# A decoder layer in split float32: two output units interleaved, weight-sum copies moved from SyncE to GpSimd, seven raw places

## The chip, the cores and the metric

The kernel runs on one core of one Trainium2 chip. The metric is the device time of one execution in microseconds (us). The core has TensorE (matmuls; PE in the profile, PEld for its weight loads), VectorE (DVE), ScalarE (ACT), GpSimd (POOL) and SyncE (SP). SyncE, ScalarE and GpSimd also issue DMAs, each in the order of its own queue; 16 DMA engines carry them out.

## What is computed

The reference is one decoder layer on 2048 tokens of width 1024, in float32:

```python
proj = rmsnorm(x, mix_norm_g) @ w_in
q, k, v, g, u = split(proj)                  # 4 heads of 128; u: 4 groups of 128 channels
y_ret  = silu(g) * head_rmsnorm(retention(rope(q), rope(k), v))
y_pool = pool_mixer(u, pool_w, pool_scale)   # trailing means over 2, 4, 8, 16 tokens, minus the token
x = x + concat(y_ret, y_pool) @ w_out
x = x + cross_attn(rmsnorm(x), mem_n, wq, wkv, wo)        # 4 heads, 256 memory tokens
x = x + conv_glu_ffn(rmsnorm(x), w_up, conv_w, w_down)    # width 2816, conv of 3
return rmsnorm(x, final_norm_g)
```

## The kernel before, in words

**Arithmetic.** Channels lie on the 128 partitions, tokens along the free axis. The tokens go in two blocks (`b` = 0, 1) of 1024, each in two halves of 512. A float32 operand is split into a high and a low part (`split`: ScalarE writes the high part at L259 or L262, VectorE the low part at L242 or L251), and each product takes three matmuls (`passes`, L267 to L269).

**Units.** `unit` (L313) makes one output tile of 128 channels: it splits a raw weight of 1024 columns into two pairs (tiles 0 to 3 and 4 to 7 of the depth), takes two PSUM banks, one for each token half, and runs four quarters of 12 matmuls: first half of the depth for both token halves, then the second, after which `evac` takes the bank away. After each quarter it draws one step of `behind[0]` (a retention or a norm running beside) and of `under[0]` (the weight sums). There are five banks. Raw weights land in `raws`, places in R and S; pairs lie in `prs`, places in Q. `new_raw` and `new_pair` use these in turn.

**Order of work.** Folded weights are computed first (the products of the attention and pooling matrices, left in Md, VWd and WPd in DRAM) while the tokens of block 0 are loaded and squared; GpSimd makes four small sums there for the memory's norm. Then, for each block: the values; the heads and pools; eight output units (L1867 on), which add to the tokens and form the next norm; the attention (16 token tiles, L856 on); eight units for its output (L1911 on), which in block 0 also load and split the tokens of block 1 (`fetch_x`, `load_x`), with the value weights of block 1 after the last. The feed-forward part runs at the end in rounds.

**Products of seven.** Block 1's heads and the whole feed-forward part multiply 2x2 blocks with seven products in place of eight. That needs sums of weight blocks, made by DMA: `weight_sums` (L939) has 42 jobs (8 in Ad for the heads, 22 in Ud, 12 in Dd). A job takes four blocks a11, a12, a21, a22 and fills d0 to d3 in DRAM: four plain copies (L950, on SyncE), then four accumulating DMAs on GpSimd: d2 += a22 and d0 += a21 (L952, L953), d1 += d2 (L956), d3 += d1 (L959). The copies are tied by `tc.issue_after(fetched[0].ins)`: they stand in SyncE's queue behind the weight load that was fetched last when they were drawn. Each `yield` is one step drawn by a unit, by an attention tile (`pace` steps, L920; `pace` is b + 1) or by the value part of block 1.

**Heads of block 1** (`head_projections`, L1514) are eight members of seven products. The last member holds pools 0 and 1; head 3's retention runs beside it. During this part R gives five raw places of 512 columns, and S is a second holder of pairs (`more`), so that there are five pairs. Finished tiles are split into `mix[k]` by `settle`: 0 to 3 are the heads, 4 to 7 the pools. Head 3's result lies in the buffer E and is split into X (part of G); tile 4 is split into a new E, which is the buffer that head 3's result leaves. The first output unit of block 1 takes the tiles in the order 7, 6, 0, 1, 2, 5, 3, 4, the others in the order 0 to 7.

**Who sets the order.** The program is fully unrolled. Each engine's queue is ordered ahead of time by a scheduler; only the last five products are ordered by hand. Dependencies are kept by semaphores, and a queue is then worked through in order.

Of the kernel before, what the change touches and what calls it, by code (L numbers as in the profile page):

```python
# [136 lines left out]
def trunk(ctx, tc, xT, memT, pos, w_qkgu, w_v, wkv, wqT, wo, wout_r, wout_p, poolT, w_up, w_dn, vecs, consts, outT):  # L137
# [16 lines left out]
    def new_e(dtype):  # L154
        return Arena(cp.tile([P, 4 * T], dtype, tag="E", name=nm("E")), 0, 4, T)

    def new_s(dtype):
        return cp.tile([P, 2 * T], dtype, tag="S", name=nm("S"))

    B = Joined(Arena(G, 16 * T, 12, T), new_e(F32R))  # L160

# [4 lines left out]
    TT = Arena(cp.tile([P, TEMPS * TW], F32, tag="T", name="T"), 0, TEMPS, TW)  # L166
    R = cp.tile([P, 3 * T], F32, tag="R", name="R")
    Q = cp.tile([P, 3 * T], F32R, tag="Q", name="Q")
    S = new_s(F32)
    raws = Places([(R, j * T) for j in range(3)] + [(S, j * T) for j in range(2)], T)  # L170
    prs = Places([(Q, j * T) for j in range(3)], T)
    vc = cp.tile([P, vecs.shape[1]], F32, tag="vecs", name="vecs")
    cs_t = cp.tile([P, consts.shape[1]], F32, tag="consts", name="consts")
# [138 lines left out]

    def unit(raw, rhs, evac, order=range(KT)):  # L313


        hs = raw if isinstance(raw, list) else pairs(raw)
        ps = [mmps() for _ in range(NS)]
        for h in range(2):
            for s in range(NS):
                for j, k in enumerate(order[4 * h : 4 * h + 4]):  # L320
                    w = [hs[k // 4][:, i, k % 4 * P : (k % 4 + 1) * P] for i in range(2)]
                    passes(ps[s], w, rhs(k, s), h + j == 0, h == 1 and j == 3)
                next(behind[0], None)
                quarter[0] += 1
                if not slow[0] or quarter[0] % 2:
                    next(under[0], None)
                if h == 1:
                    evac(s, ps[s])

    def load_tile(src, room=None):  # L330
        raw = new_raw() if room is None else room.f
# [214 lines left out]
    def fetch_x(b, k):  # L546

        out = []
        for s in range(NS):
            out.append(TT.take())  # L550
            sp.dma_start(out[s].f[:, :SUB], xT[k * P : (k + 1) * P, b * T + s * SUB : b * T + (s + 1) * SUB])
        return out

    def load_x(k, s_acc, got):
# [301 lines left out]
    def attention(sums, beside, pace):  # L856


        scl, nscl = (smp.tile([P, 8], F32, tag="scl", name=nm("scl"), bufs=2) for _ in range(2))
        low, high, far = B.arenas[0].take(KT), B.arenas[0].take(KT // 2), B.arenas[1].take(KT // 2)  # L860
        tables = [low, None, new_z(F32R).take(KT)]
        prob = [([high, far], [high.r, far.r]), ([low], [low.r[:, : 4 * T], low.r[:, 4 * T :]])]

        def load_m(hp):

            out = mw[hp]
            for kp in range(KT // 2):
                raw = new_raw()
                fetched[0] = sp.dma_start(raw.rearrange("p (k n) -> p k n", k=2), Md[hp, 2 * kp : 2 * kp + 2].rearrange("k p n -> p k n"))
                if hp == 0 and kp == 0:  # L870

                    out += [(pr[:, 0], pr[:, 1]) for pr in pairs(raw)]
                    yield
                    continue
                for i in range(2):
                    u = tables[2 * hp].r[:, (2 * kp + i) * T : (2 * kp + i + 1) * T]
                    split(raw[:, i * SUB : (i + 1) * SUB], u[:, :SUB], u[:, SUB:])
                    out.append((u[:, :SUB], u[:, SUB:]))
                yield

        def turn(pt, t, e):
            tp = aux()
            for j in range(4):
                pe.transpose(tp[:, j * P : (j + 1) * P], e.f[:, j * P : (j + 1) * P], ident)
            hi, lo = (r.rearrange("p (k t) -> p k t", t=T)[:, :, t * P : (t + 1) * P] for r in pt[1])
            turned.append(act.activation(hi, tp.rearrange("p (k t) -> p k t", k=4), AF.Copy))
            tt(dve, lo, tp.rearrange("p (k t) -> p k t", k=4), hi.bitcast(F32), ALU.subtract)
            e.free()

        turned.clear()  # L890
        mw = [[], []]
        for _ in load_m(0):
            pass
        more_m = load_m(1)
        late = []
        for i in range(2 * KT):
            hp, t = divmod(i, KT)
            ps = mmps()
            for k in range(KT):
                x2 = [X[:, 2 * k + j, t * P : (t + 1) * P] for j in range(2)]  # L900
                passes(ps, x2, mw[hp][k], k == 0, k == KT - 1)
            if i == 0:
                rn, _, _ = norm_tables(sums, wide=False)
                ts(dve, scl, rn, 1.0 / 16.0, ALU.mult)
                ts(dve, nscl, rn, -1.0 / 16.0, ALU.mult)
            mx, sm = small(2), small(2)
            dve.reduce_max(out=mx, in_=ps.rearrange("p (h m) -> p h m", h=2), axis=AX.X)
            ts(dve, mx, mx, nscl[:, t : t + 1], ALU.mult)
            e = TT.take()
            for j in range(2):  # L910
                act.activation(e.f[:, j * NMEM : (j + 1) * NMEM], ps[:, j * NMEM : (j + 1) * NMEM], AF.Exp,
                               bias=mx[:, j : j + 1], scale=scl[:, t : t + 1], accum_out=sm[:, j : j + 1])
            dve.reciprocal(sm, sm)
            for j in range(2):
                ej = e.f[:, j * NMEM : (j + 1) * NMEM]
                ts(dve, ej, ej, sm[:, j : j + 1], ALU.mult)
            if len(late) == 2:
                turn(*late.pop(0))
            late.append((prob[hp], t, e))
            for _ in range(pace):  # L920
                next(under[0], None)
            if i < KT - 2:
                next(more_m, None)
            else:
                for _ in range(pace):
                    next(beside, None)

        def end():
            for one in late:
                yield turn(*one)  # L930

        return prob, end()
# [6 lines left out]
    def weight_sums():  # L939

        jobs = [((w_qkgu[a], w_qkgu[c]), 0, 4, Ad[p]) for p, (a, c) in enumerate(PAIRS)]
        jobs += [((w_up[f], w_up[f + NF]), 0, 4, Ud[f]) for f in range(NF)]
        for at, (k0, n) in enumerate(ROUNDS):
            jobs += [((w_dn[2 * j], w_dn[2 * j + 1]), k0, n, Dd[at, j]) for j in range(KT // 2)]
        for w, k0, n, to, in jobs:
            a11, a12, a21, a22 = (block(w, i // 2, i % 2, k0, n) for i in range(4))
            d = [to[i][:, : n * P] for i in range(4)]
            with tc.issue_after(fetched[0].ins):
                for i, a in ((2, a21), (0, a11), (1, a11), (3, a12)):
                    sp.dma_start(d[i], a)  # L950
            yield
            pool.dma_start(d[2], a22, accum_op=ALU.add, max_dma_last_dim=2048)  # L952
            pool.dma_start(d[0], a21, accum_op=ALU.add, max_dma_last_dim=2048)  # L953
            yield
            yield
            pool.dma_start(d[1], d[2], accum_op=ALU.add, max_dma_last_dim=2048)  # L956
            yield
            yield
            pool.dma_start(d[3], d[1], accum_op=ALU.add, max_dma_last_dim=2048)  # L959

    class Round:

# [551 lines left out]
    def head_projections(b, v, rb, tabs, t1, t2, z3, z4):  # L1514
# [1 line left out]

        nonlocal raws, prs
        pieces, far = B.arenas[0], new_e(F32)
        more = new_s(F32R)
        raws = Places([(R, j * SUB) for j in range(5)], SUB)  # L1520
        side = Arena(R, 5 * SUB, 1, SUB).take().f
        prs = Places([(Q, j * T) for j in range(3)] + [(more, j * T) for j in range(2)], T)
        t3 = pieces.take(4)
        todo, ready, mix, gates, outs, tables = [], [], [None] * KT, {}, {}, []

# [202 lines left out]
        while ready:  # L1728
            settle(True)
        assert all(u is not None for u in mix) and far.room() == 4  # L1730
        spare = new_s(F32)
        raws = Places([(R, j * T) for j in range(3)] + [(spare, j * T) for j in range(2)], T)
        prs = Places([(Q, j * T) for j in range(3)], T)
        return mix, spare

    def rows_norm(s_acc):
        rn = smp.tile([P, 8], F32, tag="rn", name=nm("rn"), bufs=3)
# [84 lines left out]
    for b in range(NB):  # L1822
# [19 lines left out]
        else:  # L1842
# [14 lines left out]
            tabs = [TT.take() for _ in range(2)]  # L1857
            for i in range(2):
                sp.dma_start(tabs[i].f[:, :SUB], rope_d[i])
            mix, S = head_projections(b, v, rb, tabs, t1, t2, z3, z4)  # L1860
        for r in rb:
            r.free()
        slow[0] = False

        xs = [TT.take() for _ in range(NS)]
        ahead = fetch_x(b, 0)
        for n in range(KT):  # L1867
            raw = new_raw()
            sp.dma_start(raw[:, :SUB], wout_r[n].rearrange("p k c -> p (k c)"))
            fetched[0] = sp.dma_start(raw[:, SUB:], WPd[n].rearrange("p k c -> p (k c)"))  # L1870
            got, ahead = ahead, fetch_x(b, n + 1) if n + 1 < KT else None
            unit(raw, lambda k, s: [r[:, s * SUB : (s + 1) * SUB] for r in mix[k][1]], add_residual(b, n, xs, got=got), (0, 2, 3, 1, 4, 6, 7, 5) if b == 0 else (7, 6, 0, 1, 2, 5, 3, 4) if n == 0 else range(KT))
        for u, _ in mix:
            if u is not None:
                u.free()
# [21 lines left out]
        def opening(room, wv):  # L1897
# [1 line left out]
            for r in room:  # L1899
                r.free()  # L1900
            for kp in range(KT // 2):
                wv.append(value_weights(kp))
                if kp:
                    yield

# [57 lines left out]
    for _ in under[0]:  # L1963
        pass
    both[0] = False
    raws = Places([(R, j * SUB) for j in range(6)] + [(S, j * SUB) for j in range(4)], SUB)
    prs = Places([(Q, j * T) for j in range(3)] + [(B.arenas[1].t, j * T) for j in range(4)], T)
    AA = Places([(Z.t, j * (T + EDGE)) for j in range(4)], T + EDGE)
    CC = Places([(Z.t, 4 * EDGE + j * T) for j in range(4, 8)], T)
# [111 lines left out]
```

## Time and profile before

| | |
|---|---|
| three runs | 2477.16, 2478.46, 2483.21 us; median 2478.46 |
| profiled execution | 2478.89 us; its span 2477.0 us |
| mean granted TensorE clock | 0.992 |
| bytes moved by DMA | 501.56 MB, 202 GB/s |
| DMA queues, share of the 16 engines | SyncE (q1) 52.4%, GpSimd (q0) 10.8%, ScalarE (q10) 3.3% |

The span goes from the first to the last instruction. The lines of the profile name engine, line, operation, `out<-in` by the program's names, and count; `[x <-y]` is idle time of the engine before, and what ended it. SPq, POOLq and ACTq are DMA issues. A busy TensorE is not one at its peak: matmuls overlap, so the count in a window tells the rate.

### The profile page before, as it was taken

Reading aid. Unit: us, or ns where it says so; the run is one execution under the profiler, and the core shown is the slowest. Engines: PE = TensorE matmul, PEld = TensorE weight load, DVE = VectorE, ACT = ScalarE, POOL = GpSimd, SP = SyncE. Lnnn points to the kernel's source line nnn. Section 1 sums busy time; section 2 is a strip of 40 time slices with the busy share of each in tenths; the row PEclk is TensorE's granted clock in tenths of the full one; section 3 lists DMA queues with packets and bytes.
Section 4 is the critical chain, followed back from the end, with each engine's and each line's share of the span. In section 5 each row is a group of like instructions: output and inputs, shape, how many; then the busy total and the mean of one; then the engine's idle time right before and its main releaser. Section 6 shows DMA issues by size and latency. Waiting matters only on the chain.

```text
span 2477.0 us, 33287 instructions
## 1 busy us (share of the span) xinstructions
PE 2422.2 (98%) x11294; PEld 2018.0 (81%) x11294; DVE 1730.7 (70%) x2969; ACT 1283.2 (52%) x2303; POOL 206.9 (8%) x272
## 2 busy tenths in 40 slices
PE   6999999999999999999999999999999999999997
PEld 6888888878788877888888888888888888888886
DVE  8645576564676675575678876897667688867876
ACT  6333423443444443434655565665555677666663
POOL 1010111101001131200000010020000000000000
PEclk9999999999999999999999999999999999999998
DMA  8363789727748898966468665665546468768951
GB/s 315 95 167 115 222 209 244 226 51 223 219 125 199 203 258 246 250 204 249 145 198 278 210 190 158 218 222 169 161 154 216 136 223 302 246 189 280 344 171 69
DMA packets 274459, 501.56 MB, mean 202 GB/s; under 512 B 28784, under 2 KB 58096, under 8 KB 274288
## 3 DMA queue, kind: packets, MB, share of 16 engines
q1 hardware_dynamic: 225584, 428.11, 52.4%
q0 software_dynamic: 24192, 43.00, 10.8%
q10 hardware_dynamic: 24512, 28.32, 3.3%
q8 instruction: 89, 1.46, 0.2%
q14 instruction: 82, 0.67, 0.1%
HBM read 398.13 MB, written 187.17 MB: 236 GB/s over the span
## 4 chain that ended last, share of the span: by engine, by line
PE 88%; DMA 5%; DVE 4%; ACT 1%; issue 1%; SPq 0%; POOLq 0%; POOL 0%; ACTq 0%; DVEq 0%
PE mm L267 28%; PE mm L269 28%; PE mm L268 27%; DMA T<-xT 1%; DVE T L242 1%; DMA T<-Xd 1%; DVE Z L242 1%; PE aux L342 1%; PE aux L268 1%; PE aux L267 1%; PE aux L269 1%; PE aux L777 0%; DVE Q L242 0%; DMA T<-pos 0%; DMA Hd<-T 0%
## 5 line engine op out<-in xcount | busy, mean ns | idle before, releaser
L267 PE MATMUL mm<-G,Q 128*128 128x512 f32 (+1 forms) x1720 | 663.2, 386 | 23.5 <-ACT Q L259 14.6
L269 PE MATMUL mm<-G,Q 128*128 128x512 f32 (+1 forms) x1720 | 660.8, 385 | 6.3 <-DVE Q L242 6.1
L268 PE MATMUL mm<-G,Q 128*128 128x512 f32 (+1 forms) x1592 | 609.8, 383 | 0.2 <-DVE G L242 0.2
L268 PE MATMUL mm<-G,E 128*128 128x512 f32 x1084 | 421.6, 389 | 0.0
L267 PE MATMUL mm<-G,E 128*128 128x512 f32 x1084 | 420.2, 390 | 0.0
L269 PE MATMUL mm<-G,E 128*128 128x512 f32 x1084 | 419.2, 389 | 0.0
L267 PEld LDWEIGHTS mm<-G,Q 128*128 128x128 f32 x1720 | 326.6, 190 | 88.9 <-ACT Q L259 15.9
L269 PEld LDWEIGHTS mm<-G,Q 128*128 128x128 f32 x1720 | 326.4, 190 | 70.7 <-DVE Q L242 8.4
L268 PEld LDWEIGHTS mm<-G,Q 128*128 128x128 f32 x1592 | 302.1, 190 | 57.3 <-DVE G L242 1.5
L242 DVE TENSOR_TENSOR Z<-Z,mm 128x512 f32<-128x512 f32 x296 | 201.4, 681 | 101.2 <-PE mm L269 101.0
L251 DVE SCALAR_TENSOR_TENSOR Z<-Z,vecs 128x1024 f32<-128x1024 f32 x176 | 224.5, 1279 | 50.0 <-ACT Z L1104 46.4
L267 PEld LDWEIGHTS mm<-G,E 128*128 128x128 f32 x1084 | 203.5, 188 | 42.4 <-ACT Z L1186 0.3
L269 PEld LDWEIGHTS mm<-G,E 128*128 128x128 f32 x1084 | 203.5, 188 | 42.3
L268 PEld LDWEIGHTS mm<-G,E 128*128 128x128 f32 x1084 | 203.5, 188 | 42.1
L1041 ACT ACTIVATE E<-R 128x512 fp32r<-128x512 f32 (+1 forms) x165 | 101.5, 615 | 142.8 <-PE mm L268 135.3
L242 DVE TENSOR_TENSOR T<-T 128x512 f32<-128x512 f32 (+3 forms) x224 | 152.9, 688 | 23.2 <-ACT T L382 11.1
L242 DVE TENSOR_TENSOR Q<-R,Q 128x512 fp32r<-128x512 f32 x153 | 106.1, 696 | 74.5 <-ACT Q L259 50.8
L242 DVE TENSOR_TENSOR G<-T,G 128x512 fp32r<-128x512 f32 (+1 forms) x181 | 119.0, 673 | 42.5 <-ACT G L990 30.5
L1041 ACT ACTIVATE Q<-R 128x512 fp32r<-128x512 f32 (+1 forms) x157 | 96.9, 618 | 99.6 <-PE mm L268 73.8
L1104 ACT ACTIVATE Z<-Z,vecs 128x1024 f32<-128x1024 f32 x88 | 109.2, 1242 | 35.5 <-DVE Z L242 34.5
L990 ACT ACTIVATE G<-T 128x512 fp32r<-128x512 f32 x157 | 95.9, 625 | 54.5 <-DMA T<-Hd 27.3
L242 DVE TENSOR_TENSOR E<-R,E 128x512 fp32r<-128x512 f32 (+1 forms) x131 | 87.4, 671 | 51.2 <-ACT E L1041 42.3
(308 smaller groups left out, 3666.6 us busy)
## 6 DMA issues: line engine op xcount, KB each, us to landing
T<-Gd SPq DMA_DIRECT2D x168, 256.0 KB, 4.3
Gd<-Z SPq DMA_DIRECT2D x110, 256.0 KB, 2.7
R<-Ud SPq DMA_DIRECT2D x106, 256.0 KB, 2.7
Ud<-w_up SPq DMA_DIRECT2D x88, 256.0 KB, 6.1
R<-w_up SPq DMA_DIRECT2D x80, 256.0 KB, 3.0
S<-Ud SPq DMA_DIRECT2D x70, 256.0 KB, 2.8
T<-xT SPq DMA_DIRECT2D x64, 256.0 KB, 4.2
Gd<-T SPq DMA_DIRECT2D x56, 256.0 KB, 3.3
```

The costliest lines, as they stand in the source:

```text
L242: return eng.tensor_tensor(out=out, in0=a, in1=b, op=op)
L251: dve.scalar_tensor_tensor(out=out, in0=a, scalar=s, in1=b, op0=op0, op1=op1)
L267: pe.matmul(ps, lh, rh, start=start, stop=False, skip_group_check=more)
L268: pe.matmul(ps, lh, rl, start=False, stop=False, skip_group_check=more)
L269: latest[0] = pe.matmul(ps, ll, rh, start=False, stop=stop, skip_group_check=more)
L342: pe.matmul(ps[:, t : t + 1], ap, one, start=True, stop=more is None)
L990: act.activation(hi, x, AF.Copy)
L1041: act.activation(p2[:, 0, :w], self.raw[i].f[:, :w], AF.Copy)
L1104: act.activation(self.c[g].f, a[:, 2:], AF.Identity, bias=cb[:, f : f + 1], scale=cw[2][:, f : f + 1])
```

## The change

Copies and adds of a weight sum are both issued by GpSimd, with no tie to a SyncE load; up to four jobs are drawn in turn, four steps a job in place of five. The attention draws `4 - pace` steps a tile: 3 in block 0 (before: 1), 2 in block 1 (as before). S is split into two holders: during the heads of block 1 the first holds one pair (four in all), the second two raw places (seven in all). The first two output units of block 1 run together: four banks, first half of the depth for unit 0 and unit 1, then the second half; tiles in the order 6, 7, 0, 1, 2, 4, 5, 3; their weights are loaded in that order by four DMAs each; unit 0's pairs are split ahead, unit 1's second pair when its turn comes. The loads of block 1's value weights are tied behind the last token load.

```diff
-    def new_s(dtype):
-        return cp.tile([P, 2 * T], dtype, tag="S", name=nm("S"))
+    def new_s(dtype, at):
+        return cp.tile([P, T], dtype, tag=f"S{at}", name=nm("S"))
...
     def unit(raw, rhs, evac, order=range(KT)):
-        hs = raw if isinstance(raw, list) else pairs(raw)
-        ps = [mmps() for _ in range(NS)]
+        units([raw if isinstance(raw, list) else pairs(raw)], rhs, [evac], order, lambda k: k)
+
+    def units(weights, rhs, evacs, order, at):
+        ps = [[mmps() for _ in range(NS)] for _ in weights]
         for h in range(2):
-            for s in range(NS):
...
+            for hs, evac, banks in zip(weights, evacs, ps):
+                if callable(hs[h]):
+                    hs[h] = hs[h]()
+                for s in range(NS):
+                    for j, k in enumerate(order[4 * h : 4 * h + 4]):
+                        w = [hs[at(k) // 4][:, i, at(k) % 4 * P : (at(k) % 4 + 1) * P] for i in range(2)]
+                        passes(banks[s], w, rhs(k, s), h + j == 0, h == 1 and j == 3)
+                    next(behind[0], None)
+                    quarter[0] += 1
+                    if not slow[0] or quarter[0] % 2:
+                        next(under[0], None)
+                    if h == 1:
+                        evac(s, banks[s])
...
-            sp.dma_start(out[s].f[:, :SUB], xT[...])
+            fetched[0] = sp.dma_start(out[s].f[:, :SUB], xT[...])
...
-            for _ in range(pace):
+            for _ in range(4 - pace):
                 next(under[0], None)
...
-        for w, k0, n, to, in jobs:
+
+        def sums(w, k0, n, to):
             a11, a12, a21, a22 = (block(w, i // 2, i % 2, k0, n) for i in range(4))
             d = [to[i][:, : n * P] for i in range(4)]
-            with tc.issue_after(fetched[0].ins):
-                for i, a in ((2, a21), (0, a11), (1, a11), (3, a12)):
-                    sp.dma_start(d[i], a)
+            def add(at, a):
+                pool.dma_start(d[at], a, accum_op=ALU.add, max_dma_last_dim=2048)
+            for i, a in ((2, a21), (0, a11), (1, a11), (3, a12)):
+                pool.dma_start(d[i], a, max_dma_last_dim=2048)
             yield
-            pool.dma_start(d[2], a22, accum_op=ALU.add, max_dma_last_dim=2048)
-            pool.dma_start(d[0], a21, accum_op=ALU.add, max_dma_last_dim=2048)
+            add(2, a22)
+            add(0, a21)
             yield
+            add(1, d[2])
             yield
-            pool.dma_start(d[1], d[2], accum_op=ALU.add, max_dma_last_dim=2048)
-            yield
-            yield
-            pool.dma_start(d[3], d[1], accum_op=ALU.add, max_dma_last_dim=2048)
+            add(3, d[1])
+
+        live, jobs = [], [sums(*j) for j in jobs]
+        while jobs or live:
+            if jobs:
+                live.append(jobs.pop(0))
+            for g in list(live):
+                if next(g, True) is not None:
+                    live.remove(g)
+                yield
...
-        more = new_s(F32R)
-        raws = Places([(R, j * SUB) for j in range(5)], SUB)
+        more = new_s(F32R, 0)
+        raws = Places([(R, j * SUB) for j in range(5)] + [(S[1], j * SUB) for j in range(2)], SUB)
...
-        prs = Places([(Q, j * T) for j in range(3)] + [(more, j * T) for j in range(2)], T)
+        prs = Places([(Q, j * T) for j in range(3)] + [(more, 0)], T)
...
+        first = 0
+        if b:
+            first, order = 2, (6, 7, 0, 1, 2, 4, 5, 3)
+            weights, evacs = [], []
+            for n in range(first):
+                raw = new_raw()
+                r = raw.rearrange("p (k c) -> p k c", c=P)
+                for at, w in ((0, WPd[n][:, 2:4]), (2, wout_r[n][:, 0:3]), (5, WPd[n][:, 0:2]), (7, wout_r[n][:, 3:4])):
+                    fetched[0] = sp.dma_start(r[:, at : at + w.shape[1]], w)
+
+                def weight_half(h, raw=raw):
+                    pr = new_pair()
+                    split(raw[:, h * SUB : (h + 1) * SUB], pr[:, 0], pr[:, 1])
+                    return pr
+
+                weights.append([weight_half(0), lambda one=weight_half: one(1)])
+                evacs.append(add_residual(b, n, xs, got=ahead))
+                ahead = fetch_x(b, n + 1)
+            weights[0][1] = weights[0][1]()
+            units(weights, mixed, evacs, order, order.index)
+        for n in range(first, KT):
...
-                wv.append(value_weights(kp))
+                with tc.issue_after(fetched[0].ins):
+                    wv.append(value_weights(kp))
```

More of the change, by code (lines that the diff above doesn't have):

```diff
@@ L168, in trunk @@
     Q = cp.tile([P, 3 * T], F32R, tag="Q", name="Q")
-    S = new_s(F32)
-    raws = Places([(R, j * T) for j in range(3)] + [(S, j * T) for j in range(2)], T)
+    S = [new_s(F32, j) for j in range(2)]
+    raws = Places([(R, j * T) for j in range(3)] + [(r, 0) for r in S], T)
     prs = Places([(Q, j * T) for j in range(3)], T)
@@ L313, in unit @@
     def unit(raw, rhs, evac, order=range(KT)):
-        hs = raw if isinstance(raw, list) else pairs(raw)
-        ps = [mmps() for _ in range(NS)]
+        units([raw if isinstance(raw, list) else pairs(raw)], rhs, [evac], order, lambda k: k)
+    def units(weights, rhs, evacs, order, at):
+        ps = [[mmps() for _ in range(NS)] for _ in weights]
         for h in range(2):
-            for s in range(NS):
[L320 to L328, printed above, removed]
+            for hs, evac, banks in zip(weights, evacs, ps):
[11 more added lines that the diff above has]
+                        evac(s, banks[s])
     def load_tile(src, room=None):
@@ L550, in fetch_x @@
             out.append(TT.take())
-            sp.dma_start(out[s].f[:, :SUB], xT[k * P : (k + 1) * P, b * T + s * SUB : b * T + (s + 1) * SUB])
+            fetched[0] = sp.dma_start(out[s].f[:, :SUB], xT[k * P : (k + 1) * P, b * T + s * SUB : b * T + (s + 1) * SUB])
         return out
@@ L1730, in head_projections @@
         assert all(u is not None for u in mix) and far.room() == 4
-        spare = new_s(F32)
-        raws = Places([(R, j * T) for j in range(3)] + [(spare, j * T) for j in range(2)], T)
+        S[0] = new_s(F32, 0)
+        raws = Places([(R, j * T) for j in range(3)] + [(r, 0) for r in S], T)
         prs = Places([(Q, j * T) for j in range(3)], T)
-        return mix, spare
+        return mix
     def rows_norm(s_acc):
@@ L1859, in trunk @@
                 sp.dma_start(tabs[i].f[:, :SUB], rope_d[i])
-            mix, S = head_projections(b, v, rb, tabs, t1, t2, z3, z4)
+            mix = head_projections(b, v, rb, tabs, t1, t2, z3, z4)
         for r in rb:
@@ L1866, in trunk, with mixed @@
         ahead = fetch_x(b, 0)
-        for n in range(KT):
+        def mixed(k, s):
+            return [r[:, s * SUB : (s + 1) * SUB] for r in mix[k][1]]
+        first = 0
[17 more added lines that the diff above has]
+        for n in range(first, KT):
             raw = new_raw()
@@ L1871, in trunk @@
             got, ahead = ahead, fetch_x(b, n + 1) if n + 1 < KT else None
-            unit(raw, lambda k, s: [r[:, s * SUB : (s + 1) * SUB] for r in mix[k][1]], add_residual(b, n, xs, got=got), (0, 2, 3, 1, 4, 6, 7, 5) if b == 0 else (7, 6, 0, 1, 2, 5, 3, 4) if n == 0 else range(KT))
+            unit(raw, mixed, add_residual(b, n, xs, got=got), (0, 2, 3, 1, 4, 6, 7, 5) if b == 0 else range(KT))
         for u, _ in mix:
@@ L1965, in trunk @@
     both[0] = False
-    raws = Places([(R, j * SUB) for j in range(6)] + [(S, j * SUB) for j in range(4)], SUB)
+    raws = Places([(R, j * SUB) for j in range(6)] + [(r, j * SUB) for r in S for j in range(2)], SUB)
     prs = Places([(Q, j * T) for j in range(3)] + [(B.arenas[1].t, j * T) for j in range(4)], T)
```

## The prediction

> **What bounds the kernel now.** I read the page first: the engine shares, the slices, the chain that ended last.
>
> ```profile
> span 2477.0 us, 33287 instructions
> PE 2422.2 (98%) x11294; PEld 2018.0 (81%) x11294; DVE 1730.7 (70%) x2969; ACT 1283.2 (52%) x2303; POOL 206.9 (8%) x272
> DMA  8363789727748898966468665665546468768951
> PE 88%; DMA 5%; DVE 4%; ACT 1%; issue 1%; SPq 0%; POOLq 0%; POOL 0%; ACTq 0%; DVEq 0%
> ```
>
> TensorE is the bound, and 54.8 us are all it stands idle. So the change can win only where TensorE is not full, and I cut the span into stages (the view by windows; columns: length, busy time and count of PE, PEld, DVE, ACT, POOL, then granted clock, DMA share, GB/s).
>
> ```profile
> 0.00:60.00 60.00, 39.24 (x267) 37.25 (x268) 51.35 (x90) 40.93 (x62) 9.16 (x12) 0.94 0.89 316
> 25.00:60.00 35.00, 25.55 (x183) 23.86 (x182) 35.00 (x57) 28.58 (x45) 2.64 (x3) 0.90 0.86 288
> 60.00:580.00 520.00, 515.61 (x2620) 437.22 (x2619) 315.29 (x671) 196.84 (x421) 50.20 (x61) 1.00 0.61 166
> 620.00:640.00 20.00, 15.62 (x55) 11.90 (x55) 10.74 (x17) 8.02 (x14) 2.84 (x4) 0.83 1.08 272
> 640.00:913.00 273.00, 270.59 (x1337) 225.86 (x1336) 189.63 (x403) 132.30 (x273) 38.78 (x47) 1.00 0.73 193
> 913.90:936.50 22.60, 16.08 (x62) 10.76 (x61) 18.59 (x56) 9.73 (x33) 12.49 (x15) 0.77 1.07 219
> 1110.00:2440.00 1330.00, 1328.75 (x5877) 1100.09 (x5876) 1001.67 (x1441) 812.02 (x1330) 58.05 (x92) 1.00 0.64 209
> 600.00:610.00 10.00, 10.00 (x46) 1.00 1.09 280
> ```
>
> The last row (from a table of 10 us steps of TensorE alone) is the full rate: 46 matmuls in 10 us, 0.217 us each. From 1110 to 2440 us there is nothing to win. Three places are left: the start (60 us, a third of it idle), 620 to 640 us (55 matmuls where 92 would fit: 37 x 0.217 = **8.0 us lost**), and 913.9 to 936.5 us. At both later places the DMA share is over 1.
>
> **The copies move to GpSimd.** First, why they run when they do. These are rows of the timelines of SyncE and of line 736's own view:
>
> ```profile
> 42.86 0.33 SPq L332 DMA_DIRECT2D S<-w_qkgu  x1
> 43.24 2.51 SPq L950 DMA_DIRECT2D Ad<-w_qkgu  x4
> ...
> 51.00 0.33 SPq L332 DMA_DIRECT2D R<-w_qkgu  x1
> ...
> 58.21 5.49 SPq L452 DMA_DIRECT2D R<-wqT  x2
> ...
> L736 ACT ACTIVATE T<-T x8: 615/632/635, 130.3 to 305.5; 128x512 f32<-128x512 f32 x8
> ```
>
> The first copies are drawn inside the unit whose first gate result is at 130.3 us, yet they issue at 43.24 us, right behind the weight load they are tied to (`fetched[0]`). So the order in the queues isn't the order of the code: an instruction runs as early as what it depends on lets it. The copies read inputs and write scratch that nothing else has touched; the tie to a SyncE load was all that held them. The change drops the tie. I therefore expect GpSimd, idle but for four initial sums, to issue copies from the first microseconds, and the 42 jobs to run back to back from there. What that does to the loads shows where jobs and loads last met, from 592 to 640 us, beside the start, which had no sums until 43 us (view of the DMA queues in a window: packets, MB, share of 16 engines; in order 5 to 30, 592 to 640, 0 to 17 and 0 to 60 us):
>
> ```profile
> q1 hardware_dynamic: 3278, 10.09, 103.0%
> ...
> q0 software_dynamic: 2304, 4.20, 49.3%
> q1 hardware_dynamic: 3985, 7.34, 47.1%
> ...
> q1 hardware_dynamic: 2462, 5.62, 88.7%
> ...
> q1 hardware_dynamic: 7382, 18.37, 83.2%
> ```
>
> Alone, SyncE's queue moved 10.09 MB in 25 us, 404 GB/s. Beside GpSimd's queue it moved 7.34 MB in 48 us, 153 GB/s. Half of 404 is 202 GB/s; between these ends I take 178. The Trainium skill, "DMA: Bandwidth & Descriptors" (Queues, rings and completion order), says that each engine takes turns between the queues that have work, a whole packet at a time. By that rule the loads would keep half; the 47.1% agrees for time, not for bytes.
>
> *Start.* In 60 us SyncE loaded 18.37 MB, 1.05 of them the four copies: 17.3 MB. Up to 17 us I leave the 5.62 MB as they are, because GpSimd's sums wait there for ACT, as in this row, the first of four:
>
> ```profile
> 8.50 1.28 POOL L242 TENSOR_TENSOR Z<-Z 128x512 f32<-128x512 f32 x1 [8.04 <-ACT Z L414]
> ```
>
> Of the other 11.7 MB, three loads of 0.52 MB (S<-w_qkgu, R<-w_qkgu and the first R<-wqT in the rows above) serve work after 60 us. So 10.1 MB must come in the 43 us from 17 to 60. At 178 GB/s they take 57 us: **+14 us** (+7 at 202 GB/s; 33 us with 153 GB/s and nothing loaded ahead; 0 if VectorE, full from 25 to 60 us, is the real limit there). The new waits on GpSimd are the adds, each behind its copy. Behind them in its queue stand the four sums of the memory norm, for which the first norm waits; I count this inside the 14.
>
> *60 to 580 us.* The DMA view of that window:
>
> ```profile
> DMA packets 52087, 86.46 MB, mean 166 GB/s; under 512 B 4396, under 2 KB 21292, under 8 KB 52054
> ...
> q0 software_dynamic: 8919, 16.24, 20.1%
> ```
>
> Without these adds and as many bytes of copies, 54 MB are left in 520 us, 104 GB/s, under the 153. TensorE lost 4.4 us there; bursts may add half of that: **+2** (0 to +10).
>
> *620 to 640 us.* Rows of SyncE, of GpSimd and of ACT:
>
> ```profile
> 588.67 3.08 SPq L950 DMA_DIRECT2D Ud<-w_up  x5
> ...
> 605.65 2.31 SPq L950 DMA_DIRECT2D Ud<-w_up  x2
> ...
> 617.07 14.44 SPq L551 DMA_DIRECT2D T<-xT  x2
> 633.81 0.81 POOL L959 DMA_DIRECT2D Ud<-Ud  x1 [0.84 <-DMA Ud<-Ud]
> 627.06 0.72 ACT L262 ACTIVATE G<-T,vecs 128x512 fp32r<-128x512 f32 x1 [13.99 <-DMA T<-xT]
> L959 POOL DMA_DIRECT2D Ud<-Ud x22 | 18.2, 829 | 103.4 <-DMA Ud<-Ud 103.4
> ```
>
> Sixteen copies (four jobs) are issued from 588.67 to 605.65 us, ahead of and between the token loads. ACT waits 14 us for such a load; the weight split TensorE needs stands behind it in ACT's queue. The four jobs end about 640 us: 51 us, or 12.8 us a job beside other traffic. 42 jobs from the start would end near 540 us, so this jam is gone, and the new tie of the value-weight loads behind the last token load helps the same way. I take **-7** of the 8 (0 if jobs still run then). On GpSimd itself 168 more issues at 0.83 us are 139 us; its 8% becomes 14%, which nobody waits for after the start. SyncE issues 168 fewer.
>
> **The two units together.** The tail of the head stage:
>
> ```profile
> 924.42 0.63 ACT L259 ACTIVATE G<-E 128x512 fp32r<-128x512 f32 x1 [1.35 <-DVE E L251]
> 931.35 0.63 ACT L259 ACTIVATE G<-E 128x512 fp32r<-128x512 f32 x1 [1.81 <-DVE E L251]
> 932.73 1.15 ACT L259 ACTIVATE E<-Z 128x512 fp32r<-128x512 f32 x2 [0.76 <-DVE G L242]
> 934.33 1.06 PE L267 MATMUL mm<-E,Q 128*128 128x512 f32 x2
> L268 PE MATMUL mm<-G,Q 128*128 128x512 f32 x6 | 3.6, 594 | 0.2 <-DVE G L242 0.2
> L269 PE MATMUL mm<-G,Q 128*128 128x512 f32 x6 | 3.3, 546 | 0.0
> L267 PE MATMUL mm<-G,Q 128*128 128x512 f32 x6 | 3.3, 602 | 3.0 <-ACT G L259 3.0
> ```
>
> G<-E is mix tile 3 (head 3), in its two halves; E<-Z is tile 4. Tile 4 goes into the buffer that tile 3 leaves, so it is last, and TensorE reaches it at 934.33 us. The last three rows are the window's groups: 18 matmuls on G, tiles 5 and 3 of unit 0 and tile 3 of unit 1. Counting all that can run before tile 4, at 6 matmuls a tile and unit (two halves, three passes): before, unit 0 has seven tiles, and unit 1 the four of its first half: 42 + 24 = 66. After, both units have 6, 7, 0, 1, 2, and then tile 4 stands ahead of 5 and 3: 30 + 30 = 60. Pairing brings work forward, the new order takes a little more back: 6 x 0.217 = 1.3 us, and the 18 that ran in the pauses now stand behind tile 4. I take **+2** for this and a slower restart. If tile 4 came before 3 after all, 84 could run, 18 more than before: 3.9 us, with the clock -6; if the second unit's weights came late, +6. The granted clock in this window was 0.77. "TensorE: Matmul & The Clock Gate" in the Trainium skill (What's actually happening) has the clock halved when idle and freed after some 3.4 us of work; by it a restart after one long pause would cost 1.7 us. The 0.77 agrees that the clock falls here.
>
> **Small edits.** Four loads of 64 to 192 KB in place of two of 256 KB for two weights: same bytes, landed long before use; 0, or +1 if SyncE holds them back. Seven raw places and four pairs for five and five: the 2.4 us that TensorE lost from 640 to 913 us, with a calmer DMA there: **-1** (-2.4 to +1). Drawing more sums in the first attention moves nothing if they have already run; 0.
>
> Sum: 14 + 2 - 7 + 2 - 1 = **+10 us**. The profiled execution took 2478.89 us (span 2477.0), the median of the three runs is 2478.46, so the base is the same within 0.4 us: 2478.9 + 10 = **2489 us**.
>
> **Rivals.** *Not slower: the start is VectorE's.* VectorE is busy 35.00 of 35 us from 25 to 60 us. If the loads keep at least 10.1 MB / 43 us = 235 GB/s, or GpSimd's adds, waiting on their copies, hold its queue thin, the start costs nothing, and the jam's 7 and the 1 remain; the pairing decides between 2473 (+2) and 2465 (-6): about 2470. For it: loads at 10 to 30 us land some 10 us ahead of use. Against it: 404 GB/s for 25 us on end is not a queue with room. *The start is all DMA's:* 153 GB/s and nothing ahead, +33, and +10 in the next stage: 2517, say 2510 us. For it: the 7.34 MB row. *The copies don't run ahead:* if something I can't see (room in GpSimd's ring, the scheduler) keeps them near where they are drawn, the start is as before and the jam stays in part: -2, 2477 us. Against it: the 43.24 us row.
>
> **How the numbers follow.** Forecast 0.45 (its own range 2482 to 2497), VectorE's start 0.32, DMA's start 0.11, no running ahead 0.12. About 0.3%, 7.4 us, is what a measurement of this kernel can tell from no change: slower is above 2486.3, faster below 2471.5. Slower: 0.33 of the forecast and 0.11, 0.44. Faster: 0.28 of VectorE's start and 0.04 of the last, 0.32. Same: 0.24. A range of 2465 to 2505 leaves out most of the 0.11 and the low end of the 0.32, under 0.2.
>
> **What would show it.** In the profile after: GpSimd's copies in the first 10 us, its last add near 550 us; TensorE full only from about 74 us; over 90 matmuls from 620 to 640 us; a pause before the first matmul on E at the tail, with full units behind. If the first copy stands after 40 us, or TensorE is full from 60 us, the forecast is wrong; if the jobs still run at 620 us, the -7 is.

## The result, and the profile after

The changed kernel takes 2590.36 us (median of 4 runs, 2587.33 to 2591.5), the kernel before 2478.43 us beside it (4 runs): **111.9 us slower**, ratio 1.0446, 95% interval 1.0428 to 1.0464. The profiled execution took 2591.39 us. The page of after, the lines that answer to those shown of before:

```profile
span 2589.6 us, 33142 instructions
...
PE 2438.6 (94%) x11294; PEld 2029.3 (78%) x11294; DVE 1734.8 (67%) x2969; ACT 1287.2 (50%) x2303; POOL 300.1 (12%) x440
...
POOL 4454555000000000000000100010000000000000
...
DMA  9999999342353222436656856475555557867951
...
PE 85%; DMA 8%; DVE 3%; ACT 2%; ACTq 1%; issue 1%; POOL 0%; SPq 0%; POOLq 0%; DVEq 0%
```

GpSimd works in the first seven of 40 slices, and in all seven the DMA engines are full, as in only one slice after them. So the weight sums ran ahead. The DMA share of the chain that ended last went from 5% to 8%. GpSimd's timeline of after shows how (start, length, instruction, idle time before it and what ended it):

```profile
1.28 4.36 POOL L960 DMA_DIRECT2D Ad<-w_qkgu  x8 [0.83 <-POOLq L2115]
6.92 0.53 POOL L960 DMA_DIRECT2D Ad<-w_qkgu  x1 [1.29 <-DMA Ad<-w_qkgu]
...
20.32 1.36 POOL L242 TENSOR_TENSOR Z<-Z 128x512 f32<-128x512 f32 x1
...
65.42 0.73 POOL L242 TENSOR_TENSOR T<-T,Z 128x256 f32<-128x256 f32 x1
...
451.94 0.82 POOL L957 DMA_DIRECT2D Dd<-Dd  x1 [2.35 <-DMA Dd<-Dd]
```

Eight copies are issued at once from 1.28 us, and from then on most issues wait until an earlier DMA is done; the last add is issued at 451.94 us. How many are under way can be estimated from the number of DMAs and their time to landing: from 300 to 400 us GpSimd issued 81, of 192 or 256 KB, with medians of 8.8 to 11.9 us, so about 7.8 at a time. The four sums of the memory norm, at 8.50 us and after in the kernel before, stand in the same queue: the last is made at 65.42 us.

Where the time goes is read from the count of matmuls by stage (view by windows, columns as above). First before, then after:

```profile
0.00:100.00 100.00, 79.24 (x509) 73.16 (x510) 83.73 (x157) 57.42 (x91) 13.29 (x17) 0.97 0.75 239
100.00:250.00 150.00, 148.09 (x816) 128.49 (x815) 76.56 (x153) 51.29 (x115) 6.55 (x8) 1.00 0.45 127
250.00:500.00 250.00, 249.49 (x1194) 208.85 (x1193) 154.49 (x333) 92.42 (x193) 38.85 (x48) 1.00 0.85 226
```

```profile
0.00:100.00 100.00, 43.31 (x270) 40.12 (x270) 52.16 (x89) 41.52 (x62) 47.05 (x77) 0.78 1.02 341
100.00:250.00 150.00, 149.02 (x817) 130.31 (x818) 84.73 (x167) 51.67 (x104) 80.12 (x114) 0.99 1.07 272
250.00:500.00 250.00, 191.55 (x913) 159.46 (x912) 112.64 (x258) 66.08 (x153) 108.27 (x154) 0.88 0.94 243
...
620.00:640.00 20.00, 20.00 (x95) 16.50 (x94) 12.68 (x30) 9.88 (x17) 0.00 (x0) 1.00 0.21 65
```

By 500 us TensorE has run 2519 matmuls before and 2000 after. The 519 missing, at 0.217 us each, are 113 us: the whole loss. 239 (52 us) are missing at 100 us, none more are lost from 100 to 250 us, and 281 (61 us) from 250 to 500 us. (Small matmuls count here as full ones, so the us are rough.) At 620 to 640 us the jam is gone, 95 matmuls in place of 55.

The second stretch is that of the folded weights. The DMA queues from 300 to 400 us in after (packets, MB, share of 16 engines; then issues, KB, median us to landing):

```profile
q0 software_dynamic: 8879, 18.75, 79.9%
q10 hardware_dynamic: 8327, 4.14, 16.8%
...
VWd<-T ACTq DMA_DIRECT2D x16, 256.0 KB, 24.8
```

and in before from 250 to 300 us, when it made the same 16 writes of the folded value weights:

```profile
q10 hardware_dynamic: 8448, 4.20, 28.5%
...
VWd<-T ACTq DMA_DIRECT2D x16, 256.0 KB, 6.1
```

GpSimd's queue (q0) and ScalarE's (q10) pass nearly the same number of packets in these 100 us, but q0's are 2.1 KB long (18.75 MB in 8879) and q10's 0.5 KB. Four fifths of the engines' time go to q0, and a write that landed in 6.1 us needs 24.8 us. The issue itself holds ScalarE longer. The rows of the tile VWd, after and then before (duration of an issue: least, median, most ns):

```profile
L465 ACTq DMA_DIRECT2D VWd<-T x16: 366/3024/6502, 307.5 to 380.9; - x16
```

```profile
L459 ACTq DMA_DIRECT2D VWd<-T x16: 366/366/551, 253.3 to 291.2; - x16
```

The chain that ended last, within 250 to 510 us of after, goes through both:

```profile
321.81 0.58 ACT T L523
322.42 6.50 ACTq L465
328.96 0.70 ACT T L523
329.68 24.71 DMA VWd<-T
...
380.91 27.99 DMA VWd<-T
```

ScalarE empties TensorE's banks into T (L523) and writes T out; T comes free when the write has landed, and the next bank waits for ScalarE. Of this chain 24.6% are writes of VWd, 8.5% their issue, and 8.6% writes of WPd, the folded pooling weights, which hold T in the same way. TensorE's listed waits from 250 to 500 us add to 58.4 us, and 56.5 of them are for a T that ScalarE or VectorE had yet to fill. These two, in turn, waited 22 us for writes of VWd to land and 17 us for writes of WPd (6 and 3 us in before).

### The profile page after: what moved, and what is told of

Same layout as the page of the kernel before. It is cut to its first block, busy times and chain, and to the rows that moved or that the text cites. A ratio compares the mean times of both kernels' runs of the same rounds, so it can differ in the third digit from the quotient of the medians.

```text
span 2589.6 us, 33142 instructions
## 1 busy us (share of the span) xinstructions
PE 2438.6 (94%) x11294; PEld 2029.3 (78%) x11294; DVE 1734.8 (67%) x2969; ACT 1287.2 (50%) x2303; POOL 300.1 (12%) x440
## 4 chain that ended last, share of the span: by engine, by line
PE 85%; DMA 8%; DVE 3%; ACT 2%; ACTq 1%; issue 1%; POOL 0%; SPq 0%; POOLq 0%; DVEq 0%
PE mm L267 27%; PE mm L268 27%; PE mm L269 27%; DMA VWd<-T 2%; DMA Ad<-w_qkgu 2%; DMA WPd<-T 1%; DMA T<-Xd 1%; ACTq L465 1%; DMA T<-wkv 1%; DVE T L242 1%; PE aux L348 1%; PE aux L798 1%; PE aux L796 0%; PE aux L268 0%; PE aux L267 0%
## 5 line engine op out<-in xcount | busy, mean ns | idle before, releaser
L267 PE MATMUL mm<-G,Q 128*128 128x512 f32 (+1 forms) x1752 | 677.5, 387 | 32.4 <-ACT Q L259 14.4
L269 PE MATMUL mm<-G,Q 128*128 128x512 f32 (+1 forms) x1752 | 674.0, 386 | 2.4 <-DVE Q L242 2.4
L268 PE MATMUL mm<-G,Q 128*128 128x512 f32 (+1 forms) x1624 | 623.7, 384 | 1.5 <-DVE G L242 1.5
L267 PEld LDWEIGHTS mm<-G,Q 128*128 128x128 f32 x1752 | 333.9, 191 | 101.7 <-ACT Q L259 15.7
L269 PEld LDWEIGHTS mm<-G,Q 128*128 128x128 f32 x1752 | 333.5, 190 | 68.2 <-DVE Q L242 4.7
L268 PEld LDWEIGHTS mm<-G,Q 128*128 128x128 f32 x1624 | 309.7, 191 | 59.4 <-DVE G L242 2.1
```

Source lines behind the costliest of these rows:

```text
L267: pe.matmul(ps, lh, rh, start=start, stop=False, skip_group_check=more)
L268: pe.matmul(ps, lh, rl, start=False, stop=False, skip_group_check=more)
L269: latest[0] = pe.matmul(ps, ll, rh, start=False, stop=stop, skip_group_check=more)
```

## The experiments

**Theory A:** the copies on GpSimd run ahead, and its deep queue takes the DMA engines from loads and from ScalarE's writes. **Rival B:** the loss is GpSimd's own order, the four norm sums behind DMA issues. **Rival C:** GpSimd as issuer costs by itself, tied or not. **Rival D** (within A): it is the length of q0's packets that decides. Beside D stands the number of q0's DMAs under way. Each ratio is against the kernel before, run on the same chip, with its 95% interval; a difference in us is the ratio's (its part above or below 1, times 2478 us). Those of the medians differ from it by up to 2 us.

**1. Only the copies moved.** The kernel before, with this alone:

```diff
-            with tc.issue_after(fetched[0].ins):
-                for i, a in ((2, a21), (0, a11), (1, a11), (3, a12)):
-                    sp.dma_start(d[i], a)
+            for i, a in ((2, a21), (0, a11), (1, a11), (3, a12)):
+                pool.dma_start(d[i], a, max_dma_last_dim=2048)
```

> The kernel before with one thing changed: the copies are issued by GpSimd without the tie. A and B: 2580 to 2610 us, all of the loss. C: 2470 to 2485 us.

2584.48 us, ratio 1.0426 (1.041 to 1.0441): +106 us. This one edit holds nearly all of the loss; four jobs drawn in turn are not needed for it.

**2. All but that.** The changed kernel with copies on SyncE again:

```diff
-            for i, a in ((2, a21), (0, a11), (1, a11), (3, a12)):
-                pool.dma_start(d[i], a, max_dma_last_dim=2048)
+            with tc.issue_after(fetched[0].ins):
+                for i, a in ((2, a21), (0, a11), (1, a11), (3, a12)):
+                    sp.dma_start(d[i], a)
```

> The changed kernel with the plain copies of the weight sums issued by SyncE again, tied behind the weight load fetched last; pairing, seven raw places, four jobs in turn stay. If the copies running ahead cost the time (theory A), or GpSimd as the issuer of the copies does (theory B), this comes back to 2470 to 2485 us. If the paired units or the seven raw places cost it (theory C), it stays above 2550 us.

2522.59 us, ratio 1.0181 (1.016 to 1.0202): +45 us, between the two times that were expected. Of the whole change's 111 by its ratio, 66 come back, not all. I had missed that the rest of the change carries a cost of its own as soon as copies are tied to loads; experiment 8 takes that up.

**3. Copies on GpSimd, but tied.** The changed kernel; a copy of one column on GpSimd waits for the fetched load, and the job's copies stand behind it:

```diff
...
+            gate = pool.tensor_copy(mark, landed[0][:, :1])
+            with tc.issue_after(gate.ins):
                 for i, a in ((2, a21), (0, a11), (1, a11), (3, a12)):
                     pool.dma_start(d[i], a, max_dma_last_dim=2048)
```

(`landed` is the place that the load fetched last fills.)

> The changed kernel with the copies still issued by GpSimd, but each job's copies stand behind a copy of one column that waits for the weight load fetched last to land, so that they run about when they did before. A (only the time of the copies matters): 2465 to 2490 us. B (GpSimd as issuer costs): above 2530 us.

2494.04 us, ratio 1.0063 (1.0048 to 1.0078): +16 us, 4 us above the expected range of A. GpSimd still issues every copy, and 95 of 111 us are gone: this speaks for A against C.

**4. The norm sums on VectorE.** The changed kernel, each of the four lines like this:

```diff
-                tt(pool, f[:, :SUB], f[:, :SUB], f[:, SUB:], ALU.add)
+                tt(dve, f[:, :SUB], f[:, :SUB], f[:, SUB:], ALU.add)
```

> The changed kernel with the four small sums of the memory norm on VectorE, so that nothing but DMA issues stands in GpSimd's queue at the start. In the profile of the changed kernel TensorE waits 31 us once for the last of these sums. If standing behind the DMA issues is a cost of its own, 2555 to 2570 us. If the loads are late anyhow because the DMA engines are shared, the wait moves to a load: 2580 to 2592 us.

2589.77 us, ratio 1.0451 (1.0434 to 1.0469): +112 us, nothing gained. By windows:

```profile
0.00:100.00 100.00, 67.50 (x431) 63.50 (x432) 63.44 (x125) 49.77 (x79) 42.02 (x74) 0.90 1.02 349
100.00:250.00 150.00, 138.79 (x709) 118.80 (x709) 78.00 (x147) 43.41 (x89) 80.67 (x114) 0.95 1.08 276
250.00:500.00 250.00, 191.49 (x872) 157.77 (x872) 109.11 (x254) 65.44 (x151) 107.42 (x153) 0.86 0.94 238
```

The start is much better, 78 matmuls short of before (17 us) in place of 239. Then 107 and 322 are missing, and at 500 us 2012 have run, where the changed kernel had 2000. B is a true wait, the longest single one of TensorE in after (its view of waits: us in total, times, longest):

```profile
PE aux L348 <- POOL T L242: 31.2, 1, 31.2
```

But without it the end stays where it was: what TensorE gains early it loses again by 500 us, while the DMA engines are full. From 250 to 500 us it waits for T again, 58.5 us in the listed waits.

**5. Tied copies on GpSimd, nothing else changed.** The kernel before with the edit of 3:

> The kernel before with only the issuer of the copies changed: GpSimd issues them, each job's behind a copy of one column that waits for the weight load fetched last. Drawing order and steps are those of before. Theory A (the time at which the copies run costs, not who issues them): 2468 to 2483 us. Theory B (GpSimd as issuer): above 2490 us.

2483.76 us, ratio 1.0017 (1.0008 to 1.0026): +4 us, just above the 2468 to 2483 expected. The issuer hardly matters, and C is out as a cause of 106 us.

**6. Running ahead, one job at a time.** The kernel of 1, still free from the first microsecond, but each job starts with a DMA of one column out of the last result of the job before, so that no more than one job is under way:

```diff
...
+            if last is not None:
+                pool.dma_start(d[2][:, :1], last[:, :1])
+            first = pool.dma_start(d[2], a21, max_dma_last_dim=2048)
+            last = d[3]
+            with tc.issue_after(first.ins):
+                for i, a in ((0, a11), (1, a11), (3, a12)):
+                    pool.dma_start(d[i], a, max_dma_last_dim=2048)
```

> The kernel before with the copies on GpSimd, free to run ahead, but one job at a time: a job's first copy waits until the last add of the job before has landed (by a DMA of one column between them), so that the queue holds four DMAs at most and mostly one. If running ahead itself is the cost, above 2550 us. If it is the depth of GpSimd's queue (eight copies in flight without waits), the loads keep most of the engines: 2480 to 2510 us.

2485.63 us, ratio 1.003 (1.0016 to 1.0043): +7 us. GpSimd's timeline and the DMA queues from 0 to 200 us in this run:

```profile
1.26 0.71 POOL L951 DMA_DIRECT2D Ad<-w_qkgu  x1 [0.81 <-POOLq L2078]
```

```profile
q1 hardware_dynamic: 9216, 25.89, 34.9%
q0 software_dynamic: 7253, 16.53, 40.7%
```

and the queues of after in the same window:

```profile
q0 software_dynamic: 15225, 37.37, 72.8%
q1 hardware_dynamic: 8488, 23.27, 31.0%
```

The copies start as early as in after, and 98 of 106 us are gone. From 300 to 400 us about 1.6 of GpSimd's DMAs are under way by the same estimate, and the last add is issued at 1034 us (1054 in before). So the early start isn't the harm; the number of DMAs that GpSimd keeps under way is, and with it the pace at which the 42 jobs run.

**7. Shorter packets.** The kernel of 1, with the limit halved on all of GpSimd's copies and adds:

```diff
-max_dma_last_dim=2048
+max_dma_last_dim=1024
```

> The kernel before with only the untied copies on GpSimd (2584 us), and GpSimd's DMAs, copies and adds, cut into rows of 1 KB in place of 2 KB. From 300 to 400 us GpSimd's queue sent 8775 packets and ScalarE's 8331, nearly one for one, but 18.5 and 4.1 MB. If the engines give each queue one packet a turn (theory D), halving GpSimd's packets halves its bytes a turn: the VWd writes land in 12 to 18 us in place of 24.6, and the time falls to 2530 to 2565 us. If it is the bytes or the engines' time that are shared (theory E), the writes stay above 21 us and the time stays above 2575 us.

2544.59 us, ratio 1.0262 (1.0239 to 1.0286): +65 us. The queues from 300 to 400 us:

```profile
q0 software_dynamic: 10387, 15.24, 72.6%
q10 hardware_dynamic: 10271, 5.10, 19.2%
...
VWd<-T ACTq DMA_DIRECT2D x16, 256.0 KB, 14.3
```

GpSimd's packets are 1.5 KB long on average (2.1 in after); ScalarE's queue moves 5.10 MB in place of 4.14, its writes land in 14.3 us in place of 24.8, and 41 of 106 us are gone. Both figures lie where D was expected. But D is not shown: this edit also left fewer DMAs under way. Seven, not eight, were issued in the first burst, and from 300 to 400 us the estimate is 4.3 at a time (60 DMAs with medians of 6.3 to 7.4 us) in place of 7.8; the last add is issued at 574 us in place of 455. With 7.8, 4.3 and 1.6 under way the loss is 106, 65 and 7 us, so the number alone would fit as well. Nor do the queues pass packet for packet throughout: 10387 and 10271 are sums over 100 us, and from 330 to 350 us they are 2123 of q0 and 3356 of q10.

**8. The new ties alone.** The kernel before with copies on SyncE, the units paired as in 10, and the two ties of the change:

```diff
-            sp.dma_start(out[s].f[:, :SUB], xT[...])
+            fetched[0] = sp.dma_start(out[s].f[:, :SUB], xT[...])
...
-                wv.append(value_weights(kp))
+                with tc.issue_after(fetched[0].ins):
+                    wv.append(value_weights(kp))
```

> The paired units in the order 5, 3, 4 (2475.4 us) with copies, drawing and places of before, and the ties of the change that concern loads: the copies stand behind the last token load too, the value weights of block 1 behind the last token load. In the kernel before, 8 us are lost from 620 to 640 us behind 16 copies. If the token loads go ahead of the copies there, 2466 to 2470 us; if the copies only jam the next loads, 2474 to 2480 us.

2503.64 us, ratio 1.0103 (1.0086 to 1.0121): +26 us, and both expectations missed. The same kernel without the ties is the second of 9 and 10, ratio 0.999, so they cost 28 us here. Two stretches of TensorE in before, in this run, and in experiment 2 (length, busy time and count of PE, granted clock, DMA share, GB/s):

```profile
350.00:400.00 50.00, 50.00 (x238) 1.00 0.94 216
...
450.00:500.00 50.00, 50.00 (x233) 1.00 0.88 247
```

```profile
350.00:400.00 50.00, 50.00 (x239) 1.00 0.21 61
...
450.00:500.00 50.00, 40.56 (x160) 0.84 1.06 297
```

```profile
350.00:400.00 50.00, 50.00 (x238) 1.00 0.26 81
...
450.00:500.00 50.00, 38.61 (x158) 0.90 1.06 291
```

With token loads as `fetched`, no copy is issued between 309 and 397 us, because the first token load goes out at 395 us, and the DMA engines have little to do; then the copies come between the loads, the engines are full from 400 to 500 us, and 73 matmuls are missing from 450 to 500 us, about 16 of the 28 us. Experiment 2 shows the same two stretches, with 75 missing. So this tie explains part of its 45 us; the rest was not followed. In the changed kernel nothing on SyncE hangs on that tie but the value weights.

**9 and 10. The two units.** The kernel before with the paired units, tile order as in the change; then with tile 4 last:

```diff
-            first, order = 2, (6, 7, 0, 1, 2, 4, 5, 3)
+            first, order = 2, (6, 7, 0, 1, 2, 5, 3, 4)
```

(and the weights loaded in that order, by five DMAs).

> The kernel before with only the two output units of block 1 paired, tiles 6, 7, 0, 1, 2, 4, 5, 3. By the count of the prediction (66 matmuls could run before tile 4, now 60) +2 us: 2478 to 2483 us. If the work of the second unit fills the pause at the end of the heads, 2465 to 2473 us.

> The same pairing with the last three tiles as 5, 3, 4 (the weights loaded in that order, five DMAs a unit). If tile 4 is what the second half waits for, this is 2 to 5 us under the pairing with 4, 5, 3; if not, the two agree within 1 us.

Order 4, 5, 3: 2481.7 us, ratio 1.0014 (1.0004 to 1.0023), +3.5 us. Order 5, 3, 4: 2475.37 us, ratio 0.999 (0.9982 to 0.9999), -2.5 us. The window of the tail, first with 4, 5, 3, then with 5, 3, 4:

```profile
900.00:950.00 50.00, 39.62 (x190) 32.52 (x189) 31.63 (x82) 17.48 (x46) 15.77 (x19) 0.86 1.04 249
```

```profile
900.00:950.00 50.00, 44.34 (x209) 35.57 (x208) 33.17 (x84) 18.76 (x49) 17.33 (x21) 0.97 1.06 270
```

The second has 19 matmuls more behind it at 950 us, and its median is 6.3 us lower. It is the one version here that beats both kernels, if only just.

**11 and 12. Raw places and pairs.** The kernel before with S split (seven raw places, four pairs); then the same with only five raw places:

```diff
-        raws = Places([(R, j * SUB) for j in range(5)] + [(S[1], j * SUB) for j in range(2)], SUB)
+        raws = Places([(R, j * SUB) for j in range(5)], SUB)
```

> The kernel before with only S in two holders: seven raw places and four pairs during the heads of block 1. The prediction has -1 us (-2.4 to +1): 2476 to 2479.5 us. If four pairs are too few, 2482 us or more.

> The kernel before with the holder S split and four pairs in place of five during the heads of block 1, but with its five raw places: the seven raw places of the run with both are left out (the second holder stands empty in that part). The run with both took 5.7 us more than before (median 2483.34 against 2479.63), and TensorE waited there 4.6 us for the high parts of pairs at L1041, against 0.5. If the missing fifth pair is the cause, this run is as slow or a little slower: 2483 to 2488. If the two more raw places are the cause (loads that run further ahead and crowd others), it is as before: 2477 to 2481.

Seven and four: 2483.34 us, ratio 1.0023 (1.0014 to 1.0031), +5.7 us. Five and four: 2489.63 us, ratio 1.0048 (1.0032 to 1.0064), +11.9 us. The longest of TensorE's waits from 640 to 913 us (us in total, times, longest), before, seven and four, five and four:

```profile
PE mm L267 <- ACT S L1041: 1.0, 2, 0.5
PE mm L267 <- ACT Q L1041: 0.5, 1, 0.5
```

```profile
PE mm L267 <- ACT Q L1041: 4.6, 4, 2.8
```

```profile
PE aux L366 <- DVE Q L242: 4.9, 1, 4.9
PE mm L267 <- ACT Q L1041: 2.7, 4, 0.8
```

The lost pair costs about 12 us (8 to 16), the two raw places give back about 6. These waits are for a half of a pair, which ScalarE (high) or VectorE (low) writes into Q or S. The five-and-four run came out slower than either expectation, on the side of the pair.

## Why the prediction was wrong, step by step

Direction and the first half of the mechanism held: copies free of their tie run ahead from the first microseconds, share the engines with the loads, and the kernel is slower. Two terms of the sum were far too small.

**"60 to 580 us: +2" is the step that failed.** It set a mean need of 104 GB/s against the 153 that a queue had kept beside GpSimd's. What hung on the DMA was not a mean: 4.2 MB of writes by ScalarE, in packets of 0.5 KB, that hold T and with it TensorE's banks. Beside about eight of GpSimd's DMAs they moved at 41 GB/s (4.14 MB in 100 us), and 61 us of matmuls are missing from 250 to 500 us. The row used, from 592 to 640 us, is SyncE's queue with packets of 1.8 KB (7.34 MB in 3985) beside q0's of 1.8 KB; no row of ScalarE's writes was weighed. The Trainium skill, "DMA: Bandwidth & Descriptors" (Queues, rings and completion order), has each engine go from queue to queue a packet at a time. GpSimd's and SyncE's queues agree in the row below, 2530 packets against 2533. GpSimd's and ScalarE's agree only in the sum, 8879 against 8327; from 330 to 350 us they passed 1774 and 2903. The prediction read the rule as half the bytes for each, which would take packets of one length and queues that always have work.

**"Start +14"** had a rate that came true at its upper end. From 17 to 60 us of after:

```profile
q0 software_dynamic: 2530, 7.07, 52.4%
q1 hardware_dynamic: 2533, 8.72, 51.9%
```

8.72 MB in 43 us are 203 GB/s; 153 to 202 were named, and 178 taken. Wrong was to spare the first 17 us. The copies wait for nothing there, and SyncE's row of after for 0 to 17 us has 2.31 MB in place of 5.62:

```profile
q1 hardware_dynamic: 1522, 2.31, 40.8%
```

Wrong, too, was to count the norm sums "inside the 14". Experiment 4 has the start without them, 17 us; with them 52. For the end the sums don't matter, as the same experiment shows.

**"620 to 640 us: -7"** held. The 95 matmuls from 620 to 640 us, and 473 from 600 to 700 us in experiment 1 with 426 before (47, or 10 us), are of other work, since the token loads now come some 110 us later. But there, too, nothing is lost: from 500 to 950 us TensorE's listed waits add to 3.1 us in after, and before had 4.4 us from 560 to 700 us alone. That the tie of the value weights helps is not shown: in experiment 8 it won nothing.

**"Two units together +2"** held: +3.5 measured (1.0 to 5.7). Tile 4 ahead of 5 and 3 is what spoils it. The -6 was named for the case that tile 4 is ready before tile 3, with 84 matmuls ahead of the pause; that case did not come. The order 5, 3, 4 has the same 84 ahead of tile 4 by another way, and it gave 19 matmuls and 6.3 us.

**"Small edits -1"** missed: +5.7 for raws and pairs (3.5 to 7.7), beyond the +1 at which its own range ended. It looked at what there was to win and gave the fifth pair away for nothing.

The parts as measured, if they simply add: 106 (copies, with the jam's gain in it) + 3.5 + 5.7 = 115 us, against 111 (106 to 115) for the whole. Nothing is left that the ties or the faster drawing would have to explain in the changed kernel; neither was tried alone there.

**Signs named:** the first copies stood where they were said to (1.28 us). TensorE was full not from 74 but from about 100 us; the last add came at 452, not near 550 us, 10.7 us a job and not 12.8. The pause before the first matmul on E at the tail is there, 2.9 us. Of the rivals, "the start is all DMA's" was nearest in kind, but it had 33 us for the start and 10 for the next stage, where 52 and 61 were missing.

## What to carry to other kernels

Before a stream of background DMAs is set free, ask how many of them its queue will keep under way, and what each queue beside it, writes too, must move in the same stage: a mean need over a long window hid the 4.2 MB of writes that TensorE's banks hung on. A background stream may start early at little cost if it is held to one job (experiment 6); a tie that looks like a needless wait may be what paces it. And where two stages meet the same full engines, taking away the wait of the first need not win anything at the end (experiment 4). Shorter packets won 41 of 106 us, but whether by their length or by the smaller number under way is open (experiment 7).

## What the runs showed of the hardware

GpSimd issued eight DMAs of 256 KB with the packet limit at 2048, and seven at 1024, before it had to wait. ScalarE's issues of its writes took 3.02 us at the median beside GpSimd's DMAs, some 7.8 of them under way, and 0.37 before, so a starved write cost its issuer compute time as well. GpSimd's and SyncE's queues passed the same number of packets in each part of 17 to 60 us (758 and 762 up to 30 us, 861 and 859 up to 45, 911 and 912 up to 60), with 7.07 and 8.72 MB in all. For ScalarE's short packets this was not so: from 330 to 350 us they were 2903 to GpSimd's 1774.
